# Which queue loads the first pair of batches: a rotary-embedding kernel with its loads dealt out anew over SyncE and ScalarE

## The chip, the cores and the metric

The kernel runs on one core of a Trainium2 chip. The metric is the device time of one execution in microseconds (us); three runs of the kernel before took 161.34 to 161.39 us, with a median of 161.35 us. Besides, one execution was recorded by the hardware profiler; all rows and durations in this text come from it.

## What is computed

The reference is a rotary position embedding over x of shape (16, 512, 1024) in float32: 16 batches, 512 positions, 16 heads of 64 elements. In each head the first 32 elements are x1 and the last 32 are x2; cos and sin have shape (512, 32) and are shared by all batches and heads.

```python
x = x.reshape(batch, seq, num_heads, head_dim)
x1, x2 = x[..., :half_dim], x[..., half_dim:]
rotated = np.concatenate([x1 * cos - x2 * sin, x1 * sin + x2 * cos], axis=-1)
```

So every element takes two products and a sum, 33.55 MB are read and 33.55 MB are written.

## The kernel before

**Tiles and rows.** The 16 batches make ten tiles. Batches 0, 1, 14 and 15 are tiles of their own (tiles 0, 1, 8 and 9): 128 partitions with 4 positions each, 16 KB to a partition, 2 MB in all. The batches between go in pairs (tiles 2 to 7): 128 partitions, of which each holds 8 positions of one batch of the pair, 32 KB to a partition, 4 MB in all. A *row* u is one position of all partitions, 128 x 1024 elements; there are 64 rows, 4 or 8 to a tile. SBUF holds a ring of 40 rows (`RING`), which is the room of tiles 0 to 5. Tiles 6 to 9 go where an earlier tile was, once its result is stored.

**Work on a row.** VectorE multiplies the row by cos into one of three PSUM buffers (`mul`, L305). GpSimd multiplies the row, its halves swapped, by the signed sin into one of eight SBUF buffers, mostly two rows at a time (L266); the fourth row of each pair tile is multiplied by VectorE instead (L298). The sum is made in one of two ways. In three rows of each pair tile TensorE adds GpSimd's product to the PSUM buffer by two matmuls with an identity (L228), and ScalarE copies the sum back into the row's place in the ring (the evacuation, L195). In all other rows VectorE adds the two (`comb`, L316). VectorE's `mul` of a row waits until the PSUM buffer of three rows before is free, which may hang on ScalarE's evacuation; GpSimd's product waits until its buffer of eight rows before is free.

**Tables.** cos and sin are loaded once into `stage` (L178), 128 partitions of 512 B each. VectorE copies cos into PSUM (L276), before its first `mul`. ScalarE makes the signed sin of the single tiles (L186, L187), and GpSimd's first product waits for that. Two matmuls (L212) rearrange the tables for the pair tiles, and ScalarE makes the signed sin of these too (L190, L191).

**Who issues which transfer.** Only SyncE and ScalarE issue transfers, each on a queue of its own; in the profile q1 is SyncE's and q10 ScalarE's. Their order is written out by hand. SyncE (`on_sync`) issues the load of tile 1 (L157), and then the ten stores, each when all rows of its tile are added (L163). ScalarE (`on_scalar`) issues the load of tile 0, the tables, and the loads of tiles 2 to 5, all without a wait; then it prepares the tables and makes the evacuations. Between these it issues the four late loads: that of tile 6 behind row 17, of tile 7 behind row 25, and of tiles 8 and 9 behind row 33, each after a wait for the stores of what was in the place (L198): tiles 0 and 1, tile 2, and tile 3. While ScalarE waits there, its next evacuations wait too.

Of the kernel before, what the change touches and what calls it, by code (L numbers as in the profile page):

```python
# [6 lines left out]
def bass_split_heads_rope_kernel(  # L7
# [60 lines left out]
    EH = H * HD // BANK  # L68
    LEAD = 1
    LAG = 10  # L70

    with ExitStack() as stack:
        x_sb = stack.enter_context(nc.sbuf_tensor([P, RING, H, 2, HALF], fp32))
# [40 lines left out]
        def in_dram(single, pairs, t):  # L114
            b, n = tiles[t]
            return single[b] if n == R1 else pairs[:, b:b + 2, :]

        def in_sbuf(t):
            b, n = tiles[t]
            k = b * R1 % RING  # L120
            return x_sb[:, k:k + n].rearrange("p n h t d -> p (n h t d)")

        def where(u):
            t, r = rows[u]
            return t, r, u % RING
# [7 lines left out]
        def wait_added(eng, u):  # L133

            if n_pe[u]:
                eng.wait_ge(sem_a, n_pe[u])
            if n_comb[u]:
                eng.wait_ge(sem_v, n_comb[u])
# [10 lines left out]
        def stores_of(k):  # L149

            return sum(b * R1 // R2 == k for b, _ in tiles)

        def load(eng, t):
            eng.dma_start(in_sbuf(t), in_dram(x1, x2, t)).then_inc(sem_in[t], 16)  # L154

        def on_sync(sp):
            load(sp, 1)  # L157
            for u in range(NU):
                t, r, k = where(u)
                if r == tiles[t][1] - 1:  # L160
                    wait_added(sp, u)
                    k = u // R2
                    sp.dma_start(in_dram(o1, o2, t), in_sbuf(t)).then_inc(sem_out[k] if k < EARLY else sem_rest, 16)  # L163
            sp.wait_ge(sem_rest, 16 * sum(stores_of(k) for k in range(EARLY, NU // R2)))

        def on_scalar(ae):
            later = {}
            for t, (b, n) in enumerate(tiles):
                if t == 1:
                    continue  # L170
                if b * R1 + n <= RING:
                    load(ae, t)
                else:

                    later.setdefault((b * R1 - RING) // R2 * R2 + R2 - 1 + LAG, []).append(t)
                if t == 0:
                    for i, (table, sem) in enumerate(((cos, sem_cos), (sin, sem_sin))):
                        ae.dma_start(stage[:, i, :], table.rearrange("(s r) d -> s (r d)", r=R1)).then_inc(sem, 16)  # L178

            ae.wait_ge(sem_i, 2)  # L180
            ae.activation(  # L181
                pick[:], ident[:].rearrange("q (s k) -> q k s", k=2)[:, :, :, None].broadcast_to([P, 2, P // 2, 2]), COPY
            ).then_inc(sem_g, 1)
            ae.wait_ge(sem_sin, 16)
            sv = stage[:, 1, :].rearrange("s (r d) -> s r d", d=HALF)
            ae.activation(s1_sb[:, :, 0, :], sv, COPY, scale=-1.0)  # L186
            ae.activation(s1_sb[:, :, 1, :], sv, COPY).then_inc(sem_s, 1)  # L187
            ae.wait_ge(sem_t, 2)
            s2 = s2_sb[:].rearrange("p (k r) t d -> p k r t d", r=R1)
            ae.activation(s2[:, :, :, 0, :], pair_ps[:, :, 1, :, :], COPY, scale=-1.0)  # L190
            ae.activation(s2[:, :, :, 1, :], pair_ps[:, :, 1, :, :], COPY).then_inc(sem_s, 1)  # L191
            for u in range(NU):
                if PE2[u]:
                    ae.wait_ge(sem_e, n_pe[u])
                    ae.activation(xs[:, u % RING, :], t1_ps[:, u % NT1, :], COPY).then_inc(sem_a, 1)  # L195
                for t in later.get(u, ()):
                    k = (tiles[t][0] * R1 - RING) // R2
                    ae.wait_ge(sem_out[k], 16 * stores_of(k))  # L198
                    load(ae, t)
# [73 lines left out]
        def on_vector(ve):  # L273
# [49 lines left out]
            for u in range(NU + LEAD):  # L323
                if u < NU:
                    mul(u)
                if u >= LEAD and not PE2[u - LEAD]:
                    comb(u - LEAD)

        on_sync(nc.sync)
        on_scalar(nc.scalar)  # L330
        on_gpsimd(nc.gpsimd)
        on_tensor(nc.tensor)
# [34 lines left out]
```

## Time and profile before

| what | value |
|---|---|
| median of three runs | 161.35 us |
| the profiled execution, its own time | 161.41 us |
| its span, first to last instruction | 160.0 us |
| GpSimd busy | 131.6 us (82%) |
| VectorE busy | 129.6 us (81%) |
| TensorE matmuls busy | 67.4 us (42%) |
| ScalarE busy | 24.1 us (15%) |
| HBM read and written | 33.69 and 33.55 MB, 420 GB/s over the span |
| landing of tile 0 and tile 1 after their issue | 12.5 and 12.2 us |
| landing of cos and sin after their issue | 12.2 and 11.9 us |

The page cuts the span into 40 slices of 4 us; a digit gives the busy share of an engine in a slice in tenths. DMA is the mean busy share of the core's 16 DMA engines, and GB/s is what they moved. A wait is written "engine line <- what it waited for: us in total, times, longest". A row of the timeline has the start, the duration, the engine, the line and the operation; ACT is ScalarE, DVE VectorE, POOL GpSimd, SP SyncE, PE TensorE, and a q behind the name (SPq, ACTq) marks the engine's instructions that issue transfers.

### The profile page before, as it was taken

To read this page: it belongs to the slowest core of one execution; us is meant where nothing else is said; L and a number is where in the kernel's file an instruction comes from. 1 tells how busy PE (TensorE), PEld (TensorE's weight loads), DVE (VectorE), ACT (ScalarE), POOL (GpSimd) and SP (SyncE) were. 2 spreads that over 40 slices of the span, in tenths; PEclk is the share of its full clock that TensorE was granted. 3 is DMA by queue.
4 is the path that set the end of the run, shared out by engine and by line. 5 is a ranking of instruction groups with operands and counts; after the bars stand their busy time and mean duration, and the time that the engine had idled before them with its cause. 6 is when DMAs were issued, how large, how long until landed. Compare 5 with 4: busy or idle time off the path is not lost.

```text
span 160.0 us, 499 instructions
## 1 busy us (share of the span) xinstructions
PE 67.4 (42%) x94; PEld 22.9 (14%) x94; DVE 129.6 (81%) x117; ACT 24.1 (15%) x27; POOL 131.6 (82%) x41
## 2 busy tenths in 40 slices
PE   6005000906890589147601762028613892294000
PEld 1002000202220223022101220012201230130000
DVE  0006894889989998999799990999999999989920
ACT  0401100020232022202120202202220222022000
POOL 1004999999999999999999999589999999999000
PEclk9999999995579655858995699656996559758555
DMA  5999999999999999999999999999999999999997
GB/s 193 426 426 430 475 442 393 389 377 463 422 418 438 422 473 401 442 459 410 410 475 426 401 459 451 393 463 401 459 397 455 410 467 422 442 410 442 401 430 299
DMA packets 3169, 67.25 MB, mean 420 GB/s; under 512 B 352, under 2 KB 608, under 8 KB 608
## 3 DMA queue, kind: packets, MB, share of 16 engines
q1 hardware_dynamic: 1584, 35.65, 52.1%
q10 hardware_dynamic: 1584, 31.59, 46.5%
q14 instruction: 1, 0.01, 0.0%
HBM read 33.69 MB, written 33.55 MB: 420 GB/s over the span
## 4 chain that ended last, share of the span: by engine, by line
POOL 45%; DVE 18%; issue 17%; DMA 7%; PE 5%; ACT 2%; ACTq 1%; DVEq 0%
POOL t_sb L266 45%; DVE x_sb L316 9%; DVE t_ps L305 8%; DMA stage<-in_sin_dram 7%; PE t_ps L228 5%; DVE t_sb L298 2%; ACT x_sb L195 1%; ACTq L178 0%; ACTq L154 0%; ACT s_sb L186 0%; ACT s_sb L187 0%; DVEq L315 0%; DVEq L302 0%
## 5 line engine op out<-in xcount | busy, mean ns | idle before, releaser
L266 POOL TENSOR_TENSOR t_sb<-x_sb,s_sb 128x2048 f32<-128x2048 f32 (+1 forms) x35 | 130.9, 3791 | 15.4 <-ACT s_sb L187 12.9
L228 PE MATMUL t_ps<-t_sb,ident 128*128 128x512 f32 x84 | 62.6, 897 | 67.4 <-DVE t_ps L305 55.1
L305 DVE TENSOR_TENSOR t_ps<-x_sb,pair_ps 128x1024 f32<-128x1024 f32 x48 | 57.5, 1221 | 6.2 <-ACT x_sb L195 6.2
L316 DVE TENSOR_TENSOR x_sb<-t_ps,t_sb 128x1024 f32<-128x1024 f32 x43 | 52.2, 1216 | 3.6 <-POOL t_sb L266 3.6
L195 ACT ACTIVATE x_sb<-t_ps 128x1024 f32<-128x1024 f32 x21 | 21.3, 1023 | 109.1 <-PE t_ps L228 97.7
L228 PEld LDWEIGHTS t_ps<-t_sb,ident 128*128 128x128 f32 x84 | 21.0, 277 | 108.6 <-DVE t_ps L305 78.0
L305 DVE TENSOR_TENSOR t_ps<-x_sb,tab_ps 128x1024 f32<-128x1024 f32 x16 | 19.2, 1221 | 0.5 <-ACT x_sb L195 0.5
L276 DVE COPY tab_ps<-stage 128x128 f32<-128x128 f32 x1 | 0.3, 295 | 12.3 <-DMA stage<-in_cos_dram 12.3
L298 DVE TENSOR_TENSOR t_sb<-x_sb,tab_ps 128x1024 f32<-128x1024 f32 x6 | 7.3, 1210 | 0.0
L212 PE MATMUL pair_ps<-stage,pick 128*128 128x256 f32 x4 | 2.0, 667 | 9.8 <-DMA stage<-in_sin_dram 9.8
L205 PE MATMUL t_ps<-zero 128*128 128x512 bf16 x6 | 2.7, 627 | 1.3 <-DVE zero L274 1.3
L212 PEld LDWEIGHTS pair_ps<-stage,pick 128*128 128x128 f32 x4 | 1.2, 324 | 10.8 <-issue 10.6
L181 ACT ACT_TABLE_LOAD x1 | 1.3, 1283 | 4.9 <-issue 4.9
L186 ACT ACTIVATE s_sb<-stage 128x128 f32<-128x128 f32 x1 | 0.3, 310 | 7.1 <-DMA stage<-in_sin_dram 7.1
L205 PEld LDWEIGHTS t_ps<-zero 128*128 128x128 bf16 x6 | 0.7, 135 | 2.4 <-DVE zero L274 1.2
L274 DVE MEMSET zero<- 128x256 uint32 x1 | 0.3, 272 | 0.9 <-PEq L349 0.9
L190 ACT ACTIVATE s_sb<-pair_ps 128x256 f32<-128x256 f32 x1 | 0.4, 383 | 1.7 <-PE pair_ps L212 1.7
L239 POOL MEMSET ident<- 128x128 f32 x1 | 0.2, 205 | 0.3 <-POOLq L349 0.3
L181 ACT ACTIVATE pick<-ident 128x256 f32<-128x256 f32 x1 | 0.4, 416 | 0.0
L191 ACT ACTIVATE s_sb<-pair_ps 128x256 f32<-128x256 f32 x1 | 0.4, 379 | 0.0
L241 POOL TENSOR_SCALAR_AFFINE_SELECT ident<-ident 128x128 f32<-128x128 f32 x1 | 0.3, 292 | 0.1
L349 POOL MEMSET const-float32-0.0<- 128x1 f32 x1 | 0.1, 98 | 0.3 <-issue 0.3
(6 smaller groups left out, 1.0 us busy)
## 6 DMA issues: line engine op xcount, KB each, us to landing
x_sb<-in_x_dram ACTq DMA_DIRECT2D x6, 4096.0 KB, 30.5
out_dram<-x_sb SPq DMA_DIRECT2D x6, 4096.0 KB, 24.6
out_dram<-x_sb SPq DMA_DIRECT2D x4, 2048.0 KB, 14.0
x_sb<-in_x_dram ACTq DMA_DIRECT2D x3, 2048.0 KB, 22.8
x_sb<-in_x_dram SPq DMA_DIRECT2D x1, 2048.0 KB, 12.2
stage<-in_cos_dram ACTq DMA_DIRECT2D x1, 64.0 KB, 12.2
stage<-in_sin_dram ACTq DMA_DIRECT2D x1, 64.0 KB, 11.9
```

The lines of the kernel that those rows point to most:

```text
L181: ae.activation(pick[:], ident[:].rearrange("q (s k) -> q k s", k=2)[:, :, :, None].broadcast_to([P, 2, P // 2, 2]), COPY).then_inc(sem_g, 1)
L186: ae.activation(s1_sb[:, :, 0, :], sv, COPY, scale=-1.0)
L190: ae.activation(s2[:, :, :, 0, :], pair_ps[:, :, 1, :, :], COPY, scale=-1.0)
L191: ae.activation(s2[:, :, :, 1, :], pair_ps[:, :, 1, :, :], COPY).then_inc(sem_s, 1)
L195: ae.activation(xs[:, u % RING, :], t1_ps[:, u % NT1, :], COPY).then_inc(sem_a, 1)
L205: pe.matmul(t1_ps[:, k, b * BANK:(b + 1) * BANK], zero[:, 0:P], zero[:], start=True, stop=True).then_inc(sem_w, 1)
L212: pe.matmul(pair_ps[:, k].rearrange("p c r d -> p (c r d)"), pick[:, k].rearrange("q s b -> q (s b)"), stage[:].rearrange("q c f -> q (c f)"),
L228: ins = pe.matmul(t1_ps[:, u % NT1, b * BANK:(b + 1) * BANK], ident[:], t2[:, b * BANK:(b + 1) * BANK], start=False, stop=True, skip_group ...
L266: pl.tensor_tensor(t2_sb[:, u % NT2:u % NT2 + n], x_sb[:, k:k + n, :, ::-1, :], table[:, :, None, :, :].broadcast_to([P, n, H, 2, HALF]), ...
L298: ve.tensor_tensor(t2_sb[:, u % NT2, :, :, :], swapped(k), over_heads(v_ps), mult)
L305: ve.tensor_tensor(t1_ps[:, u % NT1, :].rearrange("p (h d) -> p h d", d=HALF), x_sb[:, k, :, :, :].rearrange("p h t d -> p (h t) d"), c_of ...
L316: ve.tensor_tensor(xs[:, k, :], t1_ps[:, u % NT1, :], t2_sb[:, u % NT2, :, :, :].rearrange("p h t d -> p (h t d)"), add,).then_inc(sem_v, 1)
```

## The change

The load of tile 2, the first pair of batches, moves from ScalarE to SyncE. SyncE issues it right behind the load of tile 1, ahead of its first wait. ScalarE then issues the load of tile 0, the two tables, and the loads of tiles 3, 4 and 5. Nothing else changes: on VectorE, GpSimd and TensorE the instructions and their order are the same, and so are the waits, the sizes of the transfers and the places in SBUF.

```diff
     LAG = 10
+    ON_SYNC = (1, 2)
...
         def on_sync(sp):
-            load(sp, 1)
+            for t in ON_SYNC:
+                load(sp, t)
             for u in range(NU):
...
         def on_scalar(ae):
             later = {}
             for t, (b, n) in enumerate(tiles):
-                if t == 1:
+                if t in ON_SYNC:
                     continue
                 if b * R1 + n <= RING:
                     load(ae, t)
```

## The prediction

> **What bounds the kernel now.** I read the page's slices first, then the waits of the three compute engines, then the chain of waits, the DMA queues of one stretch, and the rows of SyncE's stores. The slices come first; a digit is a tenth, a slice 4 us.
>
> ```profile
> DVE  0006894889989998999799990999999999989920
> POOL 1004999999999999999999999589999999999000
> DMA  5999999999999999999999999999999999999997
> GB/s 193 426 426 430 475 442 393 389 377 463 422 418 438 422 473 401 442 459 410 410 475 426 401 459 451 393 463 401 459 397 455 410 467 422 442 410 442 401 430 299
> ```
>
> The transfers are busy from start to end, at a mean 420 GB/s. GpSimd and VectorE start in the fourth slice and are then busy too. So two things are tight at once: what moves a byte later costs nothing if the engines still get it in time, and what starts the engines later costs, unless they have stalls to give back. The waits tell what starts them and where they stall.
>
> ```profile
> DVE tab_ps L276 <- DMA stage<-in_cos_dram: 12.3, 1, 12.3
> POOL t_sb L266 <- ACT s_sb L187: 12.9, 1, 12.9
> ACT x_sb L195 <- DMA out_dram<-x_sb: 11.4, 2, 7.0
> DVE t_ps L305 <- ACT x_sb L195: 6.7, 6, 3.7
> POOL t_sb L266 <- DVE t_ps L305: 2.4, 1, 2.4
> ```
>
> The start hangs on the **tables** cos and sin, not on x: VectorE's first copy waits for cos, GpSimd's first product for what ScalarE makes of sin. The other three rows are one later stall: ScalarE waits for stores before it may issue a refill, its next evacuations come late, VectorE and then GpSimd wait for them. The chain of waits, in order of time, begins the same way; the columns are start, duration, what.
>
> ```profile
> 1.72 11.90 DMA stage<-in_sin_dram
> 13.62 0.02 issue
> 13.64 0.31 ACT s_sb L186
> 13.95 0.21 ACT s_sb L187
> 14.16 0.07 issue
> 14.23 9.51 POOL t_sb L266 x5
> ```
>
> From 14.23 us GpSimd works without a gap up to 102.2 us. The landing of sin sets that start.
>
> **How the two queues share.** q1 is SyncE's (its 35.65 MB are the 33.55 MB of stores and one batch of 2.1 MB), q10 is ScalarE's. In the stretch from 30 to 42 us, q1 has a store of 16 KB rows (2048 KB over 128 partitions) and q10 loads of 32 KB rows. The answer on its queues:
>
> ```profile
> DMA packets 225, 5.00 MB, mean 416 GB/s; under 512 B 16, under 2 KB 16, under 8 KB 16
> ## 3 DMA queue, kind: packets, MB, share of 16 engines
> q10 hardware_dynamic: 112, 3.15, 64.4%
> q1 hardware_dynamic: 113, 1.85, 36.0%
> ```
>
> The packets are equal in number, 112 and 113, and the bytes are not, 3.15 and 1.85 MB. While both queues have work they take turns **packet by packet, whatever the size**: a queue of small packets gets few bytes.
>
> **The change, part by part.** (1) *What stands beside the tables.* The tables stay on ScalarE's queue, behind batch 0. Batches 0 and 1 have equal packets on the two queues and end together (ScalarE's batch took 12.5 us to land, SyncE's 12.2). Now SyncE's queue is empty after that, and the tables pass alone: they need about 0.4 us (sin landed at 13.6 us, batch 0 some 0.35 us before). In the changed kernel SyncE's queue goes on with the first pair, tile 2. The tables are 128 rows of 512 B each; the page counts 608 packets under 2 KB and 352 under 512 B, so 256 packets of tables, 16 to each of the 16 engines, 8 for cos and 8 for sin. Tile 2 has 128 rows of 32 KB, 8 to an engine. Taking turns, cos gives 8 packets while tile 2 gives its 8; then SyncE's queue is empty and sin passes alone. One 32 KB packet takes 32,768 B over a sixteenth of 427 GB/s (second to fourth slice, loads alone), 1.23 us; eight take 9.8 us. **Sin lands at 13.6 + 9.8 = 23.4 us, and everything that computes starts 9.8 us later**, GpSimd at 24.0 us. Tile 2 itself still lands at about 23 us, since the tables take almost no bytes from it; so it isn't late for tile 2's first product.
>
> No row of before has 512 B packets against 32 KB ones. The bounds: nothing, as now (a gain is excluded, for the tables stay behind batch 0, with which they land already); and a turn for every packet, cut off where tile 2 runs out, 9.8 us, with a turn more or less for which queue leads, 8.6 to 11.0. I take 9.8: in the nearest rows, the ones above, packets of two sizes and the 16 under 512 B count one by one.
>
> The Trainium skill speaks against this: "DMA: Bandwidth & Descriptors", Queues, rings and completion order, lets an engine drain a whole packet of typically 9 to 17 descriptors before it turns to the other queue. If the 8 rows of a table were one such packet, the delay would be two turns, 2.5 us, and the sum by it 161.4 us (the first rival below). The row of 30 to 42 us shows single rows of 16 and 32 KB taking turns, and does not show rows as small as the tables'.
>
> (2) *Issue time.* SyncE gets one more DMA instruction, ahead of its first wait. ScalarE loses one of four (they took 2.62 us together), so some 0.65 us before its table load at 4.86 us; it then waits for sin anyway (7.1 us now). Cost and gain nothing, hidden by the tables' landing. If that cover were gone, 0.65 us.
>
> (3) *The later tiles.* ScalarE's queue goes from the tables at once to tiles 3, 4, 5; tile 3 lands near 33 us, as now (between 34.8 and 36.0) or sooner, and is first needed when GpSimd reaches row 16, at 48.1 + 9.8 us. Nothing is late. SyncE's first store stands behind tile 2, which is done at 23 us, and is issued only at 24.85 + 9.8.
>
> (4) *What is given back.* The stores are later by 9.8 us at issue, but the loads go on without them, so the queues are shorter when stores come. The rows of SyncE's stores, start and duration of the issue, from tile 2 on:
>
> ```profile
> 52.64 0.63 SPq L163 DMA_DIRECT2D out_dram<-x_sb  x1
> 68.98 0.54 SPq L163 DMA_DIRECT2D out_dram<-x_sb  x1
> 86.11 0.54 SPq L163 DMA_DIRECT2D out_dram<-x_sb  x1
> 105.77 0.54 SPq L163 DMA_DIRECT2D out_dram<-x_sb  x1
> 121.61 0.54 SPq L163 DMA_DIRECT2D out_dram<-x_sb  x1
> 137.94 0.54 SPq L163 DMA_DIRECT2D out_dram<-x_sb  x1
> 153.22 0.34 SPq L163 DMA_DIRECT2D out_dram<-x_sb  x1
> ```
>
> An undisturbed tile takes 16.34 us (first step; the last of 4 MB, 16.33, agrees). Five steps to 137.94 took 85.30 us, 3.60 more than five times 16.34. That excess is ScalarE's wait: its evacuation of row 33 ended at 91.9 us, and it held the next ones until tile 3's store had landed, at 98.0 us. In the changed kernel it comes to that wait at 91.9 + 9.8 = 101.7 us. When is the store down by then? Four 4 MB loads (tiles 2 to 5, 9.8 us each) and the two 2 MB stores (4.9 each) fill the queues from 13.2 to 62.2 us. Tile 2's store is issued at 62.4 and tile 6's load at 68.4, when row 17 is evacuated (58.6 + 9.8; batch 1's store, which held that load until 59.1, is down). These two are through at 82.0. Tile 3's store is issued at 78.8, runs alone from 82.0, and tile 7's load joins it at 84.6 (row 25, 74.8 + 9.8); the store then has six of eight packets left and takes turns for them, 12 x 1.23 = 14.8 us, to 99.4, and lands within 1 us of that. So it is there over 1 us before ScalarE asks, and the **3.6 us are given back**. Bounds: 2.4 us (GpSimd's own stall, the row above) to 4.1 us (0.79 + 3.32, the two long steps alone).
>
> (5) *The end.* The last store was issued at 153.22 and the span ended at 160.0, 6.8 us. It will be issued at 153.2 + 9.8 - 3.6 = 159.4. Its 2.1 MB need 4.9 us by the rate above, and the first loads had 2.4 us around their 9.8 (12.2 to landing): 7.3 us at most; below, 6.6 if nothing stands before it. I keep 6.8.
>
> **Sum**, against the profiled execution (161.41 us with a span of 160.0; the median of the runs is 161.35, 0.06 less, and I let that go): 161.41 + 9.8 - 3.6 = **167.6 us**. The transfers then stand still for some us in all, first near 62 us and later ahead of the last 4 MB store.
>
> **The rivals.**
> *Tables pass in bundles* (the other side). Place: the tables' packets against tile 2's, from 12 to 13 us. Price: at most two turns, 2.5 us, less what ScalarE's wait gives back. That wait ends with a store whose landing hangs on bytes, not on when the engines began, so it shrinks by as much as they start later, up to 3.6 us. The point from which it decides: a delay below 3.6 us, three turns, costs nothing. Time 161.4, not slower. For it: no row shows such small packets against large ones. Against it: the equal counts.
> *The tables are not held at all, and tile 2 is late instead.* Tiles 2 and 3 share from 13.2 us, so tile 2 needs 19.6 us and lands at 32.8; GpSimd wants it at 32.4 us, 0.4 us earlier, and the first store, issued at 24.85, waits behind it on SyncE's queue until 32.8. The stores that ScalarE waits for then land up to 4 us later. Time 161.8 to 165.4. Against it: only if the tables' packets slip past.
> *The stall stays.* The start is late and nothing is given back: 161.41 + 9.8 = 171.2. For it: total bytes are the same and the transfers had no idle time. Against it: the loads run ahead for 9.8 us, and tile 3's store has over 1 us in hand, by a count that lets tile 7 in at once.
>
> **How the numbers follow.** Full delay with the stall given back 0.77; stall kept 0.04; tables in bundles 0.12; tile 2 late 0.07. The range takes 8.6 to 11.0 us for the delay, 2.4 to 4.1 for what comes back and 6.6 to 7.3 for the tail: 161.41 + 8.6 - 4.1 - 0.2 = 165.7 to 161.41 + 11.0 - 2.4 + 0.5 = 170.5. I set its low end at 165.2, which takes in the worst of the late tile 2 (0.03 of the 0.07): it holds 0.80. A difference of 0.2%, 0.32 us, is about what a measurement of this kernel can tell. Faster by more: 0.05, from the bundles with a lucky order of stores. Within: 0.07, the rest of the bundles. Slower: 0.88.
>
> **What would show it.** Sin and cos land near 23.2 us, cos after 21 us to landing instead of 12.2; tile 2 lands at the same time; GpSimd's first product starts at 24.0. The row of ScalarE waiting for stores is gone, and all 4 MB stores are 16.3 us apart. The transfers show a slice below 9 after 60 us. I am wrong if the tables land before 17 us, or if ScalarE's wait for stores is still there.

## The result, and the profile after

The changed kernel takes 166.18 us (median of six runs, 165.38 to 166.68) against 161.38 us, a ratio of 1.0288 (95% interval 1.0257 to 1.0318): **slower by 2.9%**. The profiled execution took 166.68 us with a span of 165.3 us. These are its slices, now of 4.13 us:

```profile
DVE  0000038968799999989999999999999998998940
POOL 1000019999999999999999999999999999999400
DMA  5999999999999975999989999999999999598897
GB/s 194 428 448 458 395 416 484 389 468 377 405 452 397 484 329 254 502 286 428 428 381 405 460 412 452 428 416 416 428 460 416 436 464 397 254 508 381 381 444 317
```

GpSimd and VectorE begin two slices later than before. The transfers, which were busy throughout, now have holes: at slices 15 and 16 and at slice 35. The waits that answer to those shown of before (total, times, longest, in us):

```profile
DVE tab_ps L278 <- DMA stage<-in_cos_dram: 22.0, 1, 22.0
POOL t_sb L268 <- ACT s_sb L189: 22.6, 1, 22.6
ACT x_sb L197 <- DMA out_dram<-x_sb: 2.9, 1, 2.9
DVE t_ps L307 <- ACT x_sb L197: 2.5, 6, 0.5
```

The first two were 12.3 and 12.9: both engines start 9.8 us later (GpSimd at 24.01 us, 14.23 before). ScalarE's wait for stores has shrunk from 11.4 to 2.9, VectorE waits for ScalarE never longer than 0.5 (3.7 before), and GpSimd's wait of 2.4 us for VectorE is gone. The chain of waits begins the same way, with one piece longer (start, duration, what):

```profile
1.72 21.67 DMA stage<-in_sin_dram
...
24.01 9.51 POOL t_sb L268 x5
```

Sin takes 21.67 us from its issue, 11.90 before. The queues in the stretch from 12.5 to 22 us say why; q1 is SyncE's, with tile 2, and q10 ScalarE's, with the tables:

```profile
q1 hardware_dynamic: 120, 3.77, 91.8%
q10 hardware_dynamic: 126, 0.06, 2.2%
```

The columns are packets, MB and the share of the engines' time. 120 and 126 packets, 3.77 and 0.06 MB: for each 32 KB packet of tile 2 about one 512 B packet of a table went through. The trace names no DMA engine, but each packet begins where another ends, so the packets of one engine can be chained. Such a chain shows the turns one by one: 32 KB from 14.79 to 16.00 us, a table row, 32 KB from 16.02 to 17.23, a table row, and so on, until this engine's last row of tile 2 is out at 22.17 us; then sin's eight rows follow one another within 0.2 us.

Last, the stores, start and duration of the issue, which give the engines' pace from tile 2 on:

```profile
62.42 0.61 SPq L165 DMA_DIRECT2D out_dram<-x_sb  x1
78.77 0.54 SPq L165 DMA_DIRECT2D out_dram<-x_sb  x1
95.10 0.54 SPq L165 DMA_DIRECT2D out_dram<-x_sb  x1
110.94 0.54 SPq L165 DMA_DIRECT2D out_dram<-x_sb  x1
127.28 0.54 SPq L165 DMA_DIRECT2D out_dram<-x_sb  x1
143.62 0.54 SPq L165 DMA_DIRECT2D out_dram<-x_sb  x1
158.89 0.34 SPq L165 DMA_DIRECT2D out_dram<-x_sb  x1
```

Tile 2's store is 9.78 us later than before, the last one 5.67 us: 4.11 us came back on the way. The last store took 6.4 us to the end of the span, 6.8 before. 161.41 + 9.78 - 4.11 - 0.42 = 166.66, against 166.68 measured.

### The profile page after: what moved, and what is told of

Its sections match the earlier page's. It is cut to its first block, busy times and chain, and to the rows that moved or that the text cites. A ratio compares the mean times of both kernels' runs of the same rounds, so it can differ in the third digit from the quotient of the medians.

```text
span 165.3 us, 499 instructions
## 1 busy us (share of the span) xinstructions
PE 70.8 (43%) x94; PEld 24.1 (15%) x94; DVE 129.7 (78%) x117; ACT 24.4 (15%) x27; POOL 131.5 (80%) x41
## 4 chain that ended last, share of the span: by engine, by line
DVE 39%; issue 16%; PE 15%; DMA 13%; POOL 8%; ACT 4%; ACTq 1%; DVEq 0%
DVE t_ps L307 19%; PE t_ps L230 15%; DVE x_sb L318 15%; DMA stage<-in_sin_dram 13%; POOL t_sb L268 8%; DVE t_sb L300 4%; ACT x_sb L197 4%; ACTq L180 0%; ACTq L155 0%; ACT s_sb L188 0%; ACT s_sb L189 0%; DVE tab_ps L285 0%; DVEq L317 0%; DVE tab_ps L286 0%; DVEq L304 0%
## 5 line engine op out<-in xcount | busy, mean ns | idle before, releaser
L230 PE MATMUL t_ps<-t_sb,ident 128*128 128x512 f32 x84 | 66.0, 946 | 59.9 <-DVE t_ps L307 41.6
L230 PEld LDWEIGHTS t_ps<-t_sb,ident 128*128 128x128 f32 x84 | 22.2, 293 | 103.3 <-DVE t_ps L307 71.4
L214 PEld LDWEIGHTS pair_ps<-stage,pick 128*128 128x128 f32 x4 | 1.2, 323 | 20.6 <-issue 20.4
```

The source lines that it names most:

```text
L214: pe.matmul(pair_ps[:, k].rearrange("p c r d -> p (c r d)"), pick[:, k].rearrange("q s b -> q (s b)"), stage[:].rearrange("q c f -> q (c f)"),
L230: ins = pe.matmul(t1_ps[:, u % NT1, b * BANK:(b + 1) * BANK], ident[:], t2[:, b * BANK:(b + 1) * BANK], start=False, stop=True, skip_group ...
```

## The experiments

The theory: a small packet takes a turn beside a large one of the other queue, so the tables land with tile 2; the late start costs 9.8 us, and ScalarE's wait for stores gives part back. The rivals: bundles or bytes decide, not packets; or tile 2's new place costs, not the late tables. Start is GpSimd's first product; changes are against the kernel before on the same chip.

| run | sin lands, us | start, us | time, us | against before |
|---|---|---|---|---|
| before | 13.6 | 14.2 | 161.4 | |
| changed | 23.4 | 24.0 | 166.18 | 1.0288 |
| e1, tile 3 beside the tables | 23.6 | 24.2 | 166.12 | 1.0294 |
| e2, tables behind tile 2 | 23.4 | 24.0 | 165.78 | 1.0268 |
| e3, tables first | 18.9 | 23.8 | 165.84 | 1.0272 |
| e4, 16 rows of each table | 18.4 | 19.0 | 162.42 | 1.0070 |
| e5, 32 rows of each table | 20.7 | 21.3 | 162.70 | 1.0098 |
| e6, tile 2 after sin | 13.7 | 14.3 | 161.73 | 1.0017 |
| e7, one queue for first loads | 9.0 | 9.6 | 161.34 | 0.9997 |
| e8, and late loads on SyncE | 9.1 | 9.7 | 162.75 | 1.0074 |
| e9, a table on each queue | 13.6 | 14.3 | 161.53 | 1.0003 |
| e10, changed, once more | 23.3 | 23.9 | 165.80 | 1.0282 |

**e1: another tile beside the tables.**

```diff
-    ON_SYNC = (1, 2)
+    ON_SYNC = (1, 3)
```

> Tile 3 instead of tile 2 goes behind tile 1 on SyncE's queue; tile 2 is back on ScalarE's, behind the tables. Theory (the tables take turns with whatever 32 KB packets the other queue has): tile 3's eight packets to an engine hold the tables as tile 2's did, sin lands at 23.4 us, GpSimd starts at 24.0, tile 2 lands near 33, time 166.2 us within 0.6. Rival (what costs is that tile 2 left ScalarE's queue): sin lands at 13.6, time 161.4.

Sin landed at 23.6 us and the time was 166.12 us (ratio 1.0273 to 1.0316). It isn't tile 2 that matters, but that the other queue holds 32 KB packets while the tables pass. Tile 2, back on ScalarE's queue, landed at 33.0 us, and nobody waited for it.

**e2: the tables late, without turns.** On the kernel before:

```diff
-                if t == 0:
+                if t == 2:
                     for i, (table, sem) in enumerate(((cos, sem_cos), (sin, sem_sin))):
```

> The kernel before, with the tables behind tile 2 on ScalarE's queue: no turns are taken, the tables only come late. Theory (the late tables are the whole of the change's price, and the stall given back comes with any late start): sin lands near 23.3 us, GpSimd starts near 23.9, the steps between the stores are 16.3 us, time 166.2 us within 0.6. Rival (tile 2 in the way of the first store, or the other order of loads, has a share in the price or in what came back): off by more than 0.6.

165.78 us (1.0248 to 1.0288), sin at 23.4. Late tables alone, with every load on its old queue, give the time of the changed kernel.

**e3: the tables first.** On the changed kernel:

```diff
             later = {}
+            for i, (table, sem) in enumerate(((cos, sem_cos), (sin, sem_sin))):
+                ae.dma_start(stage[:, i, :], table.rearrange("(s r) d -> s (r d)", r=R1)).then_inc(sem, 16)
             for t, (b, n) in enumerate(tiles):
...
-                if t == 0:
-                    for i, (table, sem) in enumerate(((cos, sem_cos), (sin, sem_sin))):
-                        ae.dma_start(stage[:, i, :], table.rearrange("(s r) d -> s (r d)", r=R1)).then_inc(sem, 16)
```

> The changed kernel with the tables ahead of batch 0 on ScalarE's queue. Theory (one turn for each packet): cos takes turns with batch 1 (8 packets of 0.61 us to an engine) and lands near 7.5 us, sin takes turns with tile 2 (8 of 1.23) and lands near 17, and batch 0 waits behind them and lands near 22; GpSimd starts near 22.3, time 164.4 to 165.6 us. Rival (a table passes as one bundle, or bytes count): both tables land by 4 us, batch 0 by 13.6, GpSimd starts by 13.7, time at most 161.4.

The waits of this run:

```profile
POOL t_sb L267 <- DMA x_sb<-in_x_dram: 22.4, 1, 22.4
DVE tab_ps L277 <- DMA stage<-in_cos_dram: 7.8, 1, 7.8
```

The bundles are out: 64 KB at the head of an empty queue took until 9.0 us (cos) and 18.9 us (sin), and batch 0 behind them came at 23.6 us; GpSimd now waits for x, not for the tables. All three are 1.5 to 2 us later than I wrote. Some 0.7 us of that is a slow beginning of the first transfers (batch 1, ahead of everything on SyncE's queue, landed at 8.8 us where 4.9 us of data and 2.4 around them give 8.1); the rest was not traced. The time of 165.84 us is 0.24 above my range.

**e4 and e5: fewer packets.** On the changed kernel, with 16 and then 32 in place of N; `sem_f` is a new semaphore, and the wait for it cost nothing (ScalarE issued cos at 1.25 us, 1.24 in the changed kernel):

```diff
...
+                        if i == 0:
+                            ae.wait_ge(sem_f, 1)
-                        ae.dma_start(stage[:, i, :], table.rearrange("(s r) d -> s (r d)", r=R1)).then_inc(sem, 16)
+                        ae.dma_start(stage[0:N, i, :], table.rearrange("(s r) d -> s (r d)", r=R1)[0:N, :]).then_inc(sem, 16)
...
+            ve.memset(stage[:], 1.0).then_inc(sem_f, 1)
             ve.memset(zero[:], 0.0).then_inc(sem_z, 1)
```

> The changed kernel, but of each table only 16 of its 128 rows are loaded, one packet to an engine; the other rows are filled with ones, so most of the output has other factors than the reference's. Theory (a turn for every packet, the semaphore's too): four turns instead of eight ahead of sin, 4 x 1.23 = 4.9 us, sin lands near 18.1 us, GpSimd starts near 18.7; most of the 4.5 us comes back in ScalarE's wait, time 161.5 to 163.0 us. Rival (the tables wait for all of tile 2, however many packets they have): sin lands at 23.2, time 166.

> As with 16 rows, but 32 of the 128 rows of each table are loaded, two packets to an engine; the other rows are ones. Theory: six turns ahead of sin, 6 x 1.23 = 7.4 us, sin lands near 20.6 us, GpSimd starts near 21.2, time 163.6 to 164.8 us. Rival (the tables wait for all of tile 2): sin at 23.2, time 166.

Sin landed at 18.4 us with one row to an engine and table, at 20.7 with two, against 23.4 with eight: the count of turns (18.1, 20.6) to within 0.3 us. Each transfer ends with one packet more on every engine, of 4 bytes, and in e4's packets this one takes a turn like a row: 32 KB, a row of cos, 32 KB, 4 bytes, 32 KB, a row of sin, 32 KB, 4 bytes. So there are four turns in e4 and six in e5. The delay (4.8, 7.1 and 9.8 us) follows the turns (four, six and eight) and not the bytes, which are an eighth and a quarter of the full tables'. Neither table waits for all of tile 2 (28.1 and 25.5 us, later than in the changed kernel, as tile 3 joins it sooner). The times are 162.42 us (1.0039 to 1.0101) and 162.70 us (1.0073 to 1.0123). The second is 0.9 us below what I wrote; its profiled execution, with 163.84 us, was inside. So more came back of a start that is 7.1 us late than I reckoned; the last point of the next section has a better count.

**e6: tile 2 waits for sin.** On the changed kernel:

```diff
             for t in ON_SYNC:
+                if t == 2:
+                    sp.wait_ge(sem_sin, 16)
                 load(sp, t)
```

> The changed kernel, but SyncE waits for sin's landing before it issues tile 2's load. Theory: the tables pass alone, sin lands at 13.6 us, GpSimd starts at 14.2; tile 2 then shares with tiles 3 and 4, comes 4 us or more after its issue to its first packet and needs 19.6 us, so it lands near 37, where GpSimd wants it at 32.4: a stall of about 5 us there, part of it given back, time 162.4 to 166.4 us. Rival (the late tables were not the cause of the late start): GpSimd starts at 24.

The start is back at 14.3 us. Tile 2 landed at 37.7 us, and GpSimd stood for 5.3 us at 32.5 us for it, both as written. The time, 161.73 us (1.0005 to 1.0030), is below my range: nearly all of the 5.3 us came back. The late loads went out at 62.6, 78.8 and 98.2 us, each on the landing of its store, against 59.1, 78.6 and 98.0 before: the transfers set the last two, and engines that come later only wait less for them.

**e7 and e8: an earlier start.** e7 has all first loads on ScalarE's queue; e8 moves the late loads to SyncE besides:

```diff
-    ON_SYNC = (1, 2)
+    ON_SYNC = ()
```

```diff
                     sp.dma_start(in_dram(o1, o2, t), in_sbuf(t)).then_inc(sem_out[k] if k < EARLY else sem_rest, 16)
+                    for v in {2: (6,), 3: (7,), 4: (8, 9)}.get(t, ()):
+                        j = (tiles[v][0] * R1 - RING) // R2
+                        sp.wait_ge(sem_out[j], 16 * stores_of(j))
+                        load(sp, v)
...
-                for t in later.get(u, ()):
-                    k = (tiles[t][0] * R1 - RING) // R2
-                    ae.wait_ge(sem_out[k], 16 * stores_of(k))
-                    load(ae, t)
```

> All first loads on ScalarE's queue: tile 0, the tables, tile 1, tiles 2 to 5; SyncE issues stores alone. Theory (with nothing on the other queue batch 0 takes 4.9 us instead of 9.8 and the tables pass at once): sin lands near 8.0 us, GpSimd starts near 8.6, 5.6 us sooner than before; but the transfers were already busy throughout the kernel before, so ScalarE's waits for stores grow by most of it, time 160.0 to 161.4 us. Rival (the engines are the bound, and the start counts in full): 155.8 us.

> As with one queue for the first loads, and the four late loads are issued by SyncE behind the stores of tiles 2, 3 and 4, so that ScalarE never waits for stores. Theory: GpSimd starts near 8.6 us and ScalarE's wait is gone, the transfers alone bound the end, time 159.6 to 161.0 us. Rival (ScalarE's wait and the start are what the time hangs on): 161.4 - 5.6 - 4.1 = 151.7 us.

e7 starts 4.6 us sooner and takes 161.34 us, the same (0.9988 to 1.0006). GpSimd stands where it gained: 7.2 us for x and 2.1 us for VectorE, in four places. In e8 ScalarE never waits for stores, and the last store is issued 9.2 us sooner than before:

```profile
144.06 0.35 SPq L165 DMA_DIRECT2D out_dram<-x_sb  x1
```

It ends with the span all the same, at 161.6 us: the last four stores land at 142.2, 151.9, 156.7 and 161.6, a store's data time apart. So engines that start 4.5 us sooner and never stall are done 9.2 us sooner, and the transfers hold the end; ScalarE's wait in the kernel before is a symptom of that. Why e8 is even slower (162.75 us, 1.0050 to 1.0097, above my range) stays open: its packets show one DMA engine alone at work for some 0.8 us at the end, and I did not find what put it behind.

**e9: a table on each queue.** On the changed kernel; sin stays on ScalarE's queue behind tile 0:

```diff
             for t in ON_SYNC:
                 load(sp, t)
+                if t == 1:
+                    sp.dma_start(stage[:, 0, :], cos.rearrange("(s r) d -> s (r d)", r=R1)).then_inc(sem_cos, 16)
...
-                    for i, (table, sem) in enumerate(((cos, sem_cos), (sin, sem_sin))):
-                        ae.dma_start(stage[:, i, :], table.rearrange("(s r) d -> s (r d)", r=R1)).then_inc(sem, 16)
+                    ae.dma_start(stage[:, 1, :], sin.rearrange("(s r) d -> s (r d)", r=R1)).then_inc(sem_sin, 16)
```

> The changed kernel, but cos goes on SyncE's queue, between tile 1 and tile 2, and sin stays on ScalarE's behind tile 0. Tile 2 stays on SyncE's queue. Theory: small packets now take turns with small ones, both tables pass in some 0.4 us, sin lands at 13.6 us and GpSimd starts at 14.2; tile 2 shares with tile 3 and lands near 33, 0.6 us after GpSimd wants it, which ScalarE's wait absorbs: time 161.2 to 162.0 us. Rival (tile 2 on SyncE's queue costs by itself): GpSimd starts at 14.2 and the time is still above 163.

> The changed kernel once more, on the chip of the split tables, for comparison. Both theories: 165.4 to 166.7 us, GpSimd starts at 24.0. If the steps between its 4 MB stores follow TensorE's clock, those with 4 matmuls of row 3 of the tile in 1.98 us take 15.8 us, those with 3.79 us take 16.3.

e9 takes 161.53 us (0.9994 to 1.0012), with tile 2 still on SyncE's queue, while the changed kernel on the same chip takes 165.80 (1.0259 to 1.0306). Table rows that face table rows pass at once. Tile 2 landed at 33.3 us, GpSimd waited 1.0 us for it, and that too came back. No version beat the kernel before.

## Why the prediction was right, step by step

- **The tables' delay**, predicted 9.8 us from equal packet counts at 30 to 42 us: 9.77. The Trainium skill has it that an engine typically drains 9 to 17 descriptors before it turns ("DMA: Bandwidth & Descriptors", Queues, rings and completion order). That isn't what these runs show: the rows went one by one, in the changed kernel and in e4 and e5.
- **Tile 2 and tile 3 not late**: tile 2 landed at 23.0 us, tile 3 at 32.9; both as predicted.
- **What is given back**, predicted 3.6 us (2.4 to 4.1): 4.11, at the far end. Two parts of the step were wrong. First, ScalarE's wait is not gone, which the prediction itself had named as a sign of being wrong. Tile 3's store landed at 102.9 us, not by 100.4; I let each transfer begin with its issue, but tile 2's store began 1.3 us after it and the loads of tiles 6 and 7 and tile 3's store 4.7 to 5.3 us after it. ScalarE waited from 101.0 to 102.9 us, and it cost nothing: its next evacuation ended at 104.9, and VectorE was busy until 105.2 and went on without a gap, as the rows at the end of this section show. That is 0.3 us of slack which I had not counted, so that the stall came back in full there is luck. Second, 16.34 us is not *the* undisturbed tile; see the last section.
- **The last store**, predicted 6.8 us with 6.6 to 7.3 as bounds: 6.4, below both. Its first row went at 159.73 us, when tile 8's store had sent its last by 159.62; before, the two stores overlapped by 0.6 us. So nothing was ahead of it, and my price for that case, 6.6, was 0.2 too high.
- **The sum**, predicted 167.6 us: the profiled execution took 166.68, 0.5 for what came back and 0.4 for the tail, and it was the slowest of six; the median lies 0.5 lower.
- **The rivals.** Bundles: e3, e4 and e5 rule them out. Tile 2's place: e1, e2 and e9. Its price as a late tile was overrated: e6 has it 5.3 us late for 0.35 us. The stall that stays: excluded by the stores' steps.
- **What a late start costs** isn't its delay less a fixed sum. Without the stall (5.1 us, counted in the last section) the engines of the kernel before would issue the last store at 148.1 us; with 6.4 us for it and the 1.4 us that the execution's time lies above its span, they would end at 155.9 us. The transfers end at 161.4. By this count, made after the runs, a start up to 5.5 us late should be free, and a later one end at 155.9 plus its delay: 163.0 us for 7.1 us (e5: 162.70), 165.4 for 9.5 (e3: 165.84), 165.7 for 9.8 (165.78 to 166.18). For 4.8 us this gives 161.4, and e4 took 162.42: where the two ends nearly meet, the later of them is too little. There the stall was not all gone: one of e4's store steps is still 17.55 us, with the matmuls that go with 15.84 (last section), and its last store took 7.0 us. e6, with 5.3 us, took 161.73; e7, 4.6 us early, 161.34.

ScalarE's evacuation behind its wait, and VectorE's work beside it, in the changed kernel:

```profile
103.86 1.03 ACT L197 ACTIVATE x_sb<-t_ps 128x1024 f32<-128x1024 f32 x1 [2.86 <-DMA out_dram<-x_sb]
104.00 1.21 DVE L318 TENSOR_TENSOR x_sb<-t_ps,t_sb 128x1024 f32<-128x1024 f32 x1
105.13 2.35 DVE L307 TENSOR_TENSOR t_ps<-x_sb,pair_ps 128x1024 f32<-128x1024 f32 x2
```

## What to carry to other kernels

In these runs two queues with work took turns by packets, so a small transfer with many short rows should not stand opposite large rows: its landing then hangs on the other queue's row size, and 64 KB came 9.8 us later here. Look at what each queue holds opposite the transfer that everything waits for; put small ones opposite an empty queue or opposite each other. The Trainium skill ("DMA: Bandwidth & Descriptors", Issuing engines are not separate DMA queues) has it that issuing from several engines only saves issue time; between e9 and e10 the queue of one 64 KB table makes 4.3 us. And where the transfers are busy throughout, a later start costs little as long as the engines still end before the transfers (4.8 us late cost 1.0 us in e4, 9.8 us late 4.3 to 4.8): work out both ends before pricing a stall (here about 155.9 and 161.4 us).

## What the runs showed beside

A tile's step at the stores is 15.8 or 16.3 us, by TensorE's clock. Here is the granted clock of the changed kernel by slices, in tenths, and then its matmuls for row 3 of tiles 4 and 5, in this order (start, duration, engine); with eight merged, the first four took 3.8 us:

```profile
PEclk9955555555955795579556759985598558957655
84.41 6.22 PE L230 MATMUL t_ps<-t_sb,ident 128*128 128x512 f32 x8 [0.74 <-DVE t_ps L307]
100.75 1.98 PE L230 MATMUL t_ps<-t_sb,ident 128*128 128x512 f32 x4 [0.80 <-DVE t_ps L307]
```

The first four fall where half the clock was granted (slice 21; 0.50 from 84.41 to 88.20 us), and the store steps from 78.77 to 95.10; the second where all of it was (slice 25; 1.00 from 100.75 to 102.73 us), and the step is 95.10 to 110.94, 15.84. ScalarE's evacuation comes later with slow matmuls, and VectorE waits 0.4 to 0.5 us for it. In e10, where this was written down ahead, all six steps agree: 15.8, 16.35, 15.8, 16.0, 16.3, 16.3 with the four matmuls in 1.98, 3.8, 1.98, 1.98, 3.8 and 3.8 us. So a tile whose engines are the bound has two paces, and where the clock's phases fall moves the time by some 0.5 us for a tile. That may be behind the changed kernel's spread of 1.3 us over its six runs, which isn't shown: their mean clock doesn't order them (0.801 in the run of 165.38 us, 0.804 in that of 166.60). It also corrects the count of the stall: by these paces ScalarE's wait cost before 17.13 - 15.84 = 1.3 and 19.66 - 15.84 = 3.8 us, 5.1 in all, of which the changed kernel returned 4.1 and lost 1.0 to slower clock phases.
